# A hybrid attention and DeltaNet block on one core: f32 probabilities times values, and four value projections as seven half-size products

## The chip, the core and the metric

The kernel runs on one core of a Trainium2 chip. The core has five engines with instruction streams of their own: TensorE (PE in the profile; its weight loads are PEld), VectorE (DVE), ScalarE (ACT), GpSimd (POOL) and SyncE (SP). TensorE multiplies a stationary operand (`lhsT`, loaded first) with a moving one (`rhs`) and adds the result into a bank of PSUM; VectorE and ScalarE bring results from there to SBUF. The engines wait for one another through semaphores, and transfers run on DMA queues that SP, ACT and POOL issue.

The metric is the device time of one execution in microseconds. It is compared by the median of several runs.

## The reference

One layer with two token mixers side by side, on 1024 tokens of width 1024. The part that the change touches is mixer A, the dilated windows of attention. Three groups of eight heads (head width 64) have windows and dilations (128, 1), (512, 4) and (2048, 16); in each group the tokens of one residue are cut into blocks of 128 queries, which look at their own block of keys and the one before.

```python
proj = h @ w_in[layer]                       # q, k, v of three groups, gates, and mixer B's inputs
...
scores = jnp.einsum('brnqhd,brnkhd->brnhqk', qb, kb) * (dh ** -0.5)
...
m = jnp.max(scores, axis=-1, keepdims=True)
p = jnp.exp(scores - m)
den = jnp.sum(p, axis=-1, keepdims=True)
o = jnp.einsum('brnhqk,brnkhd->brnqhd', p / den, vb)
lse = (m + jnp.log(den))[..., 0].transpose(0, 1, 2, 4, 3)
...
wts = jax.nn.softmax(jnp.stack(lses), axis=0)
o = jnp.einsum('gbsh,gbshd->bshd', wts, jnp.stack(outs))
```

Mixer B is a gated delta rule with a short convolution, evaluated in chunks. Both outputs are gated, projected up, merged, projected once more and added to the input; a final RMSNorm follows. Everything is float32.

## The kernel before

**Products from f16 parts.** TensorE's operands in the projections are pairs of f16 tensors: a high part and a low part that holds what the high one leaves over. A product takes three passes, high by high, high by low and low by high (`mm3_steps`, lines 183 to 185). The normalised input is `h_hi` and `h_lo`, times 16; weights are `whi` and `wlo`, times 256, made by ScalarE (high) and VectorE (low) from a staged f32 block.

**Units.** The columns of the input projection are cut into units of 256 columns. Attention has 18: for each of three groups `g` (0: undilated, 1: dilation 4, 2: dilation 16, which is worked as residues of 8 with a mask) and two half sets of four heads `hs`, one for queries, one for keys, one for values. A `Feed` object yields a unit's matmuls in steps and prepares the next unit's weights ahead. A `Normal` unit has 32 steps. A `Seven` unit (28 steps) writes its product as two by two blocks and takes seven products of half blocks instead of eight: the four weight blocks are combined into seven (`Seven.split`: sums by VectorE at line 329, splits at lines 330 and 331), the combined inputs are kept once (`sums`), and partial results are copied between PSUM banks (line 367) or kept in SBUF (`x7`) and subtracted as the blocks come out. `SEVENS` lists the units that are done so: before the change, queries and keys of groups 1 and 0, three gate units and four `z` units.

**A value unit** (`v_unit`) has tokens on the partitions: `h` is stationary and the weights move, 256 columns at a time (`gen`). Each PSUM bank is brought out as `Vh` (ScalarE, line 730) and `Vl` (VectorE, line 731), both f16 and scaled to 16 times the value. There is a `gen7` with `by_token` too, which no unit uses before the change: there a product has four groups of tokens, each with 4 × 3 passes of 128 columns.

**Attention** (`att_run`) goes through a set (`g`, `hs`) in 16 steps, one for each block of queries and parity of heads, two heads in each. Three stages are staggered by a step each. `scores` multiplies queries and keys (lines 790 and 792); VectorE adds the mask and takes the row's extreme (line 799), ScalarE the exponential with its sum (line 803), which leaves probabilities in f32 (`sm`). `turn` transposes them on TensorE (line 813), one 128×128 piece for each head and key block, and splits them into `th` (ScalarE, line 818) and `tl` (VectorE, line 819, in the profile under the helper's line 86). `values` multiplies them with the values, three passes of 64 columns for each head and key block. A step has one key block (`nk` = 1) in group 2 and at the start of a residue, two elsewhere. Between the stages TensorE's program takes steps of the feed, as many as the pace gives, so that projections of the next set fill the time in which the other engines work on the present one. The order of TensorE's program is as written; the other engines' is put in order by the planner, by priority.

**Merging.** Results of groups 2 and 1 go to DRAM; for group 0 `combine` reads them back, weighs the three and divides by their common denominator and by the factor 16 of the values (line 885).

**After attention** come mixer B's preparation (from about 545 us), its scan over chunks with the `z` units between, and the output projections.

```python
PE.matmul(out, lhsT=th[:, c], rhs=Vh[:, b, vs], start=(hd == 0 and i == 0), stop=False,
          skip_group_check=True)
PE.matmul(out, lhsT=th[:, c], rhs=Vl[:, b, vs], start=False, stop=False,
          skip_group_check=True)
PE.matmul(out, lhsT=tl[:, c], rhs=Vh[:, b, vs], start=False, stop=(i == nk - 1),
          skip_group_check=True)
```

Of the kernel before, what the change touches and what calls it, by code (L numbers as in the profile page):

```python
# [18 lines left out]
S = 1024  # L19
# [3 lines left out]
H_SCALE = 16.0  # L23
W_SCALE = 256.0
P_SCALE = 1.0 / (H_SCALE * W_SCALE)
# [8 lines left out]
def att_unit(g, hs, what):  # L34
    return U_ATT + (g * 2 + hs) * 3 + what


def gdn_unit(hb, what):
# [2 lines left out]

RUNS = 32
RUNS7 = 28
SEVENS = ([att_unit(g, hs, w) for g in (1, 0) for hs in range(2) for w in range(2)]
          + [U_GATE + i for i in (0, 6, 7)] + [U_Z + i for i in range(4)])
SOLVE_LATER = 1500
SILU = ((1, 2), (0, 0), (1, 0))
# [30 lines left out]
def hybrid_block(ctx: ExitStack, tc: tile.TileContext, A):  # L78
    nc = tc.nc
    V, SC, PE, GP = nc.vector, nc.scalar, nc.tensor, nc.gpsimd  # L80

    def STT(out, in0, scalar, in1, op0, op1, eng=None):
        (eng or V).scalar_tensor_tensor(out, in0, scalar, in1, op0=op0, op1=op1)  # L83

    def TT(out, in0, in1, op, eng=None):
        (eng or V).tensor_tensor(out, in0, in1, op)  # L86
# [9 lines left out]
    start = [ctx.enter_context(ExitStack()) for _ in range(2)]  # L96
# [399 lines left out]
    with tc.manual_schedule(engines={nc.vector.engine, nc.scalar.engine}):  # L496
# [8 lines left out]
        pts = turn_rows(0)  # L505
# [27 lines left out]
        pts = turn_rows(3)  # L533
# [45 lines left out]
    ap = att.enter_context(tc.tile_pool(name="att", bufs=1, side="right"))  # L579
# [15 lines left out]
    def rope_room():  # L595
        return rp.tile([128, 2, 512], F32, name="rx", tag="rx", bufs=2)
# [37 lines left out]
    def rope_tiles():  # L634
        return {n: rp.tile([128, 2, S], F16, name=f"pc{n}", tag=f"pc{n}", bufs=1) for n in "hl"}
# [31 lines left out]

    def rope_first(g, ws, pieces):

        pts = [rope_tiles(), {n: ap.tile([128, 2, S], F16, name=f"pk{n}", tag="V" + n, bufs=2) for n in "hl"}]  # L670

        def half(pt, banks, hf, *offset):
            x = rope_room()
            for ct, p in enumerate(banks):
                rope_evict(g, x, p, ct, *offset)
            rope_half(g, pt, hf, x, *offset)

        for pt, banks in zip(pts, qk):
            half(pt, banks, 0, 0)
        ab = [q, [bank("S", 2), bank("S", 2)]]  # L680
        for i, u in ((2, 1), (3, 0), (3, 1)):
            for ct in range(2):
                quarter(ab[u][ct], ws[u], ct, i)
            if u == 0:

                with tc.high_priority():
                    for n in range(2):
                        feed.units[0][1].split(n)
        for pt, banks in zip(pts, ab):
            half(pt, banks, 1)  # L690
        for pt, pc in zip(pts, pieces):
            rope_out(pt, pc)
# [16 lines left out]

    def v_unit(g, tiles):  # L710
        def start():
            vs = [ap.tile([128, 8, 256], F16, name=n, tag=n, bufs=2) for n in ("Vh", "Vl")]
            tiles().extend(vs)
            return vs

        def gen(w):
            wh, wl = w
            Vh, Vl = start()
            for jj in range(4):
                p = bank("mm", 3)  # L720
                for u in range(2):
                    j = 2 * jj + u
                    for i, _ in enumerate(mm3_steps(
                            p[:, u * 256:u * 256 + 256], (lambda k: tok(g, h_hi, k, j), lambda k: tok(g, h_lo, k, j)),
                            (lambda k: wh[:, k], lambda k: wl[:, k]), first=(u == 0))):
                        if u == 1 and i == KT - 1:
                            with tc.high_priority():
                                vh = Vh[:, 2 * jj:2 * jj + 2].rearrange("p a b -> p (a b)")
                                vl = Vl[:, 2 * jj:2 * jj + 2].rearrange("p a b -> p (a b)")
                                SC.activation(vh, p, AF.Copy, scale=H_SCALE * P_SCALE)  # L730
                                STT(vl, p, H_SCALE * P_SCALE, vh, ALU.mult, ALU.subtract)
                        if i % 2:
                            yield

        def gen7(w):
            vs = start()

            def out(c, hf, p, rest):
                cs = slice(128 * c, 128 * c + 128)
                vh, vl = [v[:, 4 * hf:4 * hf + 4, cs] if g == 0 else  # L740
                          v.rearrange("p (r h) c -> p r h c", h=2)[:, :, hf, cs] for v in vs]
                p = p.rearrange("p (i c) -> p i c", c=128)
                with tc.high_priority():
                    if rest is not None:
                        rest = rest.rearrange("p (i c) -> p i c", c=128)
                        x = rope_room()[:, 0].rearrange("p (i c) -> p i c", c=128)
                        STT(x, p, -1.0, rest, ALU.mult, ALU.subtract)
                        p = x
                    SC.activation(vh, p, AF.Copy, scale=H_SCALE * P_SCALE)
                    STT(vl, p, H_SCALE * P_SCALE, vh, ALU.mult, ALU.subtract)  # L750

            yield from seven_products(w, out, by_token(g))

        return gen, gen7
# [2 lines left out]

    def att_run(g, hs, ts, pace):

        Qh, Ql, K, Vh, Vl = ts  # L760
        steps = [(j, par) for j in range(8) for par in range(2)]
        osbs, Ps, ths, pos = {}, {}, {}, {}
        if (g, hs) == sets[-1]:

            room = ap.tile([128, 2048], F32, name="osbs", tag="Ks", bufs=2)
# [40 lines left out]
        def turn(s):  # L806
            nk = len(blocks(steps[s][0]))
            P = Ps.pop(s)
            pt = bank("G", 2)
            for u in range(2):  # L810
                for i in range(nk):
                    c = (u * nk + i) * 128
                    PE.transpose(pt[:, c:c + 128], P[:, u, i * 128:i * 128 + 128], ident)  # L813
            n = 256 * nk
            th = ap.tile([128, 512], F16, name="th", tag="th", bufs=2)
            tl = ap.tile([128, 512], F16, name="tl", tag="tl", bufs=2)
            with tc.high_priority():
                SC.copy(th[:, :n], pt[:, :n])  # L818
                TT(tl[:, :n], pt[:, :n], th[:, :n], ALU.subtract)
            ths[s] = th, tl  # L820

        def values(s):
            j, par = steps[s]
            kb = blocks(j)
            nk = len(kb)
            th, tl = ths.pop(s)
            if par == 0:
                pos[j] = bank("O", 1)
            po = pos[j]
            for u in range(2):  # L830
                hd = 2 * u + par
                out = po[:, hd * 64:hd * 64 + 64]
                vs = slice(hd * 64, hd * 64 + 64)
                for i, b in enumerate(kb):
                    c = slice((u * nk + i) * 128, (u * nk + i) * 128 + 128)
                    PE.matmul(out, lhsT=th[:, c], rhs=Vh[:, b, vs], start=(hd == 0 and i == 0), stop=False,
                              skip_group_check=True)
                    PE.matmul(out, lhsT=th[:, c], rhs=Vl[:, b, vs], start=False, stop=False,
                              skip_group_check=True)
                    PE.matmul(out, lhsT=tl[:, c], rhs=Vh[:, b, vs], start=False, stop=(i == nk - 1),  # L840
                              skip_group_check=True)
            if par == 0:
                return
            osb = osbs.pop(j)
            SC.copy(osb[:, :256], po[:, :256])
            if g == 1:
                dst = dram[g, hs].rearrange("(n r) c -> r n c", r=4)[j // 2, 128 * (j % 2):128 * (j % 2) + 128]
                nc.scalar.dma_start(out=dst, in_=osb)
            elif g == 2:
                nc.scalar.dma_start(out=dram[g, hs].rearrange("(n r) c -> r n c", r=8)[j], in_=osb)  # L850
            else:
                feed.later(TURN_LAG, combine(hs, j, osb))

        n = len(steps)
# [11 lines left out]
    def combine(hs, j, osb):  # L866
# [8 lines left out]
        f = ap.tile([128, 3, 4], F32, name="f", tag="f", bufs=2)  # L875
        mx = ap.tile([128, 3, 4], F32, name="mx", tag="mx", bufs=2)
# [5 lines left out]
        TT(mx[:, 1], sml[:, 0], sml[:, 1], ALU.add)  # L882
        TT(mx[:, 1], mx[:, 1], sml[:, 2], ALU.add)
        V.reciprocal(mx[:, 2], mx[:, 1])
        STT(f, f, 1.0 / H_SCALE, mx[:, 2:3].to_broadcast([128, 3, 4]), ALU.mult, ALU.mult)

        def hv(x):
            return x.rearrange("p (h v) -> p h v", v=64)
# [88 lines left out]
    tiles = {}  # L977
# [695 lines left out]
    for t in range(8):  # L1673
# [373 lines left out]
```

## Time and profile before

| what | value |
|---|---|
| median of 3 runs | 1074.25 us (1074.08 to 1074.3) |
| the profiled execution's own time | 1076.42 us |
| its span on the core | 1074.6 us |
| mean granted clock of TensorE | 0.997 |
| from HBM, to HBM | 91.13 MB, 36.90 MB |

The profile is of one execution, so sums made from its rows stand beside 1076.42 us. An instruction's group is shown by its line, engine, operation and the tiles that it writes and reads; a `x` number is a count of instructions. Durations of matmuls overlap, since TensorE starts the next before the last has ended, and their ends are modelled: the pace of a stream is read from the starts. A line can be a helper's: 83 and 86 are the kernel's short forms for VectorE operations, so there the tiles tell the group. "Idle before" is idle time of an engine just ahead of an instruction, with what ended it.

### The profile page before, as it was taken

Reading aid. Unit: us, or ns where it says so; the run is one execution under the profiler, and the core shown is the slowest. Engines: PE = TensorE matmul, PEld = TensorE weight load, DVE = VectorE, ACT = ScalarE, POOL = GpSimd, SP = SyncE. Lnnn points to the kernel's source line nnn. Section 1 sums busy time; section 2 is a strip of 40 time slices with the busy share of each in tenths; the row PEclk is TensorE's granted clock in tenths of the full one; section 3 lists DMA queues with packets and bytes.
Section 4 is the critical chain, followed back from the end, with each engine's and each line's share of the span. In section 5 each row is a group of like instructions: output and inputs, shape, how many; then the busy total and the mean of one; then the engine's idle time right before and its main releaser. Section 6 shows DMA issues by size and latency. Waiting matters only on the chain.

```text
span 1074.6 us, 23700 instructions
## 1 busy us (share of the span) xinstructions
PE 1048.8 (98%) x9410; PEld 640.7 (60%) x9410; DVE 864.8 (80%) x1986; ACT 560.9 (52%) x1274; POOL 56.3 (5%) x107
## 2 busy tenths in 40 slices
PE   7999999999999999999999999999999999999997
PEld 5994685775956855765645545555555555444444
DVE  6997997869879779979966997986488679899844
ACT  6455766566666656547735733234344346343523
POOL 0000000000000000000000000110200000000000
PEclk9999999999999999999999999999999999999999
DMA  8144531632625432641234357786685433763132
GB/s 278 60 133 103 139 104 54 171 98 87 181 69 154 108 103 63 177 115 46 76 123 165 84 130 205 237 240 164 184 267 174 140 99 116 286 209 123 48 131 79
DMA packets 99776, 148.47 MB, mean 138 GB/s; under 512 B 31168, under 2 KB 64704, under 8 KB 98512
## 3 DMA queue, kind: packets, MB, share of 16 engines
q1 hardware_dynamic: 69264, 84.64, 27.3%
q0 software_dynamic: 12320, 44.11, 13.1%
q10 hardware_dynamic: 18080, 18.20, 4.9%
q8 instruction: 74, 1.21, 0.5%
q14 instruction: 38, 0.31, 0.1%
HBM read 91.13 MB, written 36.90 MB: 119 GB/s over the span
## 4 chain that ended last, share of the span: by engine, by line
PE 60%; DVE 27%; ACT 5%; issue 3%; DMA 3%; SPq 1%; ACTq 0%; DVEq 0%
PE ps_mm L183 14%; PE ps_mm L184 14%; PE ps_mm L185 14%; DVE ca L83 4%; DVE wlo L83 2%; DVE X L86 2%; DVE stmp L86 2%; DVE sm L799 2%; PE ps_S L185 2%; PE ps_S L184 2%; PE ps_S L183 2%; DVE tl L86 1%; PE ps_G L813 1%; DVE rt L86 1%; ACT sm L803 1%
## 5 line engine op out<-in xcount | busy, mean ns | idle before, releaser
L185 PE MATMUL ps_mm<-h_hi,wlo 128*128 128x512 f16 (+1 forms) x552 | 207.9, 377 | 0.0
L183 PE MATMUL ps_mm<-h_hi,whi 128*128 128x512 f16 (+1 forms) x492 | 185.5, 377 | 0.0
L184 PE MATMUL ps_mm<-h_lo,whi 128*128 128x512 f16 (+1 forms) x492 | 185.3, 377 | 0.0
L185 PEld LDWEIGHTS <-wlo 128*128 128x128 f16 x788 | 77.2, 98 | 86.5 <-issue 0.7
L183 PEld LDWEIGHTS <-whi 128*128 128x128 f16 x848 | 83.3, 98 | 69.1 <-issue 0.6
L184 PEld LDWEIGHTS <-whi 128*128 128x128 f16 x848 | 83.1, 98 | 67.9 <-issue 0.9
L183 PE MATMUL ps_mm<-whi,h_hi 128*128 128x256 f16 x384 | 105.1, 274 | 0.0
L185 PE MATMUL ps_mm<-whi,h_lo 128*128 128x256 f16 x384 | 104.7, 273 | 0.0
L184 PE MATMUL ps_mm<-wlo,h_hi 128*128 128x256 f16 x384 | 104.7, 273 | 0.0
L803 ACT ACTIVATE sm<-sm,osb 128x128 f32<-128x128 f32 (+1 forms) x160 | 69.5, 435 | 65.3 <-DVE osb L799 58.7
L86 DVE TENSOR_TENSOR tl<-ps_G,th 128x256 f16<-128x256 f32 (+1 forms) x96 | 51.8, 539 | 22.1 <-ACT th L818 21.6
L799 DVE CUSTOM_DVE_ANT_0 sm<-ps_S,amask 128x128 f32<-128x128 f32 (+1 forms) x192 | 59.2, 345 | 6.0 <-PE ps_S L792 5.9
L83 DVE SCALAR_TENSOR_TENSOR wlo<-wstage,whi 128x1024 f16<-128x1024 f32 x50 | 60.9, 1217 | 3.4 <-ACT whi L166 3.2
L83 DVE SCALAR_TENSOR_TENSOR ca<-xc,cw,ca 128x512 f32<-128x512 f32 x72 | 53.8, 747 | 5.5 <-ACT ca L1010 4.8
L166 ACT ACTIVATE whi<-wstage 128x1024 f16<-128x1024 f32 x49 | 51.4, 1051 | 1.7 <-ACT gst L948 0.8
L813 PE MATMUL ps_G<-cons,sm 128*128 128x128 f32 x280 | 47.9, 275 | 3.2 <-ACT sm L803 1.5
L83 DVE SCALAR_TENSOR_TENSOR whi<-wstage,whi 128x512 f16<-128x512 f32 x60 | 40.8, 687 | 12.3 <-ACT whi L330 11.7
L330 ACT ACTIVATE whi<-wstage 128x512 f16<-128x512 f32 x60 | 37.1, 626 | 19.6 <-DVE wstage L329 13.3
L813 PEld LDWEIGHTS ps_G<-cons,sm 128*128 128x128 f32 x280 | 35.5, 141 | 19.4 <-ACT sm L803 5.0
L184 PEld LDWEIGHTS <-h_hi 128*128 128x128 f16 x384 | 45.8, 119 | 1.6
L183 PE MATMUL ps_mm<-h_hi,wlo 128*128 128x512 f16 x120 | 45.6, 380 | 1.0 <-DVE rx L83 1.0
L183 PEld LDWEIGHTS <-h_hi 128*128 128x128 f16 x384 | 45.5, 119 | 1.5
(459 smaller groups left out, 2595.7 us busy)
## 6 DMA issues: line engine op xcount, KB each, us to landing
wstage<-in_w POOLq DMA_DIRECT2D x68, 512.0 KB, 4.5
og<-osb ACTq DMA_DIRECT2D x32, 132.0 KB, 2.2
og<-og SPq DMA_DIRECT2D x32, 132.0 KB, 2.2
gspb<-gst ACTq DMA_DIRECT2D x16, 256.0 KB, 2.4
sga<-gspa SPq DMA_DIRECT2D x8, 512.0 KB, 6.5
wstage<-in_w_up POOLq DMA_DIRECT2D x8, 512.0 KB, 4.7
wos<-in_w_out SPq DMA_DIRECT2D x8, 512.0 KB, 5.3
sgb<-gspb SPq DMA_DIRECT2D x8, 512.0 KB, 4.9
```

Of the source, the lines that this page charges most:

```text
L83: (eng or V).scalar_tensor_tensor(out, in0, scalar, in1, op0=op0, op1=op1)
L86: (eng or V).tensor_tensor(out, in0, in1, op)
L166: in_turn(SC.activation(hi[:, 4 * c:4 * c + 4], st, AF.Copy, scale=W_SCALE))
L183: PE.matmul(out, lhsT=wh(k), rhs=mh(k), start=first and i == 0, stop=False, skip_group_check=True)
L184: PE.matmul(out, lhsT=wh(k), rhs=ml(k), start=False, stop=False, skip_group_check=True)
L185: last_pe[0] = PE.matmul(out, lhsT=wl(k), rhs=mh(k), start=False, stop=last and i == len(ks) - 1, skip_group_check=True).ins.name
L330: in_turn(SC.activation(t[:, b, 0], self.part[name], AF.Copy, scale=W_SCALE))
L799: V.tensor_tensor_reduce(P[:, u, :128 * nk], psc[:, u * 256:u * 256 + 128 * nk], mask, -cexp, -NEG, ALU.add, ALU.min, accum_out=osb[:, 256 ...
L803: SC.activation(P[:, u, :128 * nk], P[:, u, :128 * nk], AF.Exp, bias=osb[:, 256 + hd:257 + hd], scale=-1.0, accum_out=osb[:, 260 + hd:261 ...
L813: PE.transpose(pt[:, c:c + 128], P[:, u, i * 128:i * 128 + 128], ident)
```

## The change

The values and the turned probabilities are kept in f32, each as one tensor, and their product is one f32 matmul for each head and key block instead of three f16 passes. The split into `Vh` and `Vl` and that into `th` and `tl` are gone; the scale 1/4096 of the projections goes into the last factor of `combine`. The value units of groups 1 and 0, four in all, join the list `SEVENS`. The memory of `pk`, used once at the start, is now a view of a `vals` buffer, as it was of `Vh` and `Vl` buffers.

```diff
-SEVENS = ([att_unit(g, hs, w) for g in (1, 0) for hs in range(2) for w in range(2)]
+SEVENS = ([att_unit(g, hs, w) for g in (1, 0) for hs in range(2) for w in range(3)]
           + [U_GATE + i for i in (0, 6, 7)] + [U_Z + i for i in range(4)])
...
-        pts = [rope_tiles(), {n: ap.tile([128, 2, S], F16, name=f"pk{n}", tag="V" + n, bufs=2) for n in "hl"}]
+        pk = ap.tile([128, 8, 256], F32, name="pk", tag="vals", bufs=2).rearrange("p a b -> p (a b)").bitcast(F16)
+        pk = pk.rearrange("p (l a s) -> p l a s", l=2, a=2)
+        pts = [rope_tiles(), {n: pk[:, i] for i, n in enumerate("hl")}]
...
-            vs = [ap.tile([128, 8, 256], F16, name=n, tag=n, bufs=2) for n in ("Vh", "Vl")]
-            tiles().extend(vs)
-            return vs
+            v = ap.tile([128, 8, 256], F32, name="vals", tag="vals", bufs=2)
+            tiles().append(v)
+            return v
...
-                                SC.activation(vh, p, AF.Copy, scale=H_SCALE * P_SCALE)
-                                STT(vl, p, H_SCALE * P_SCALE, vh, ALU.mult, ALU.subtract)
+                                SC.copy(v[:, 2 * jj:2 * jj + 2].rearrange("p a b -> p (a b)"), p)
...
                 with tc.high_priority():
-                    if rest is not None:
-                        rest = rest.rearrange("p (i c) -> p i c", c=128)
-                        x = rope_room()[:, 0].rearrange("p (i c) -> p i c", c=128)
-                        STT(x, p, -1.0, rest, ALU.mult, ALU.subtract)
-                        p = x
-                    SC.activation(vh, p, AF.Copy, scale=H_SCALE * P_SCALE)
-                    STT(vl, p, H_SCALE * P_SCALE, vh, ALU.mult, ALU.subtract)
+                    if rest is None:
+                        SC.copy(dst, p)
+                    else:
+                        STT(dst, p, -1.0, rest.rearrange("p (i c) -> p i c", c=128), ALU.mult, ALU.subtract)
...
-            th = ap.tile([128, 512], F16, name="th", tag="th", bufs=2)
-            tl = ap.tile([128, 512], F16, name="tl", tag="tl", bufs=2)
+            PT = ap.tile([128, 512], F32, name="PT", tag="PT", bufs=2)
             with tc.high_priority():
-                SC.copy(th[:, :n], pt[:, :n])
-                TT(tl[:, :n], pt[:, :n], th[:, :n], ALU.subtract)
-            ths[s] = th, tl
+                SC.copy(PT[:, :n], pt[:, :n])
+            PTs[s] = PT
...
-                    PE.matmul(out, lhsT=th[:, c], rhs=Vh[:, b, vs], start=(hd == 0 and i == 0), stop=False,
-                              skip_group_check=True)
-                    PE.matmul(out, lhsT=th[:, c], rhs=Vl[:, b, vs], start=False, stop=False,
-                              skip_group_check=True)
-                    PE.matmul(out, lhsT=tl[:, c], rhs=Vh[:, b, vs], start=False, stop=(i == nk - 1),
+                    PE.matmul(out, lhsT=PT[:, c], rhs=vals[:, b, vs], start=(hd == 0 and i == 0), stop=(i == nk - 1),
                               skip_group_check=True)
...
-        STT(f, f, 1.0 / H_SCALE, mx[:, 2:3].to_broadcast([128, 3, 4]), ALU.mult, ALU.mult)
+        STT(f, f, P_SCALE, mx[:, 2:3].to_broadcast([128, 3, 4]), ALU.mult, ALU.mult)
```

More of the change, by code (lines that the diff above doesn't have):

```diff
@@ L711, in start @@
         def start():
-            vs = [ap.tile([128, 8, 256], F16, name=n, tag=n, bufs=2) for n in ("Vh", "Vl")]
-            tiles().extend(vs)
-            return vs
+            v = ap.tile([128, 8, 256], F32, name="vals", tag="vals", bufs=2)
+            tiles().append(v)
+            return v
         def gen(w):
             wh, wl = w
-            Vh, Vl = start()
+            v = start()
             for jj in range(4):
@@ L727, in gen @@
                             with tc.high_priority():
-                                vh = Vh[:, 2 * jj:2 * jj + 2].rearrange("p a b -> p (a b)")
-                                vl = Vl[:, 2 * jj:2 * jj + 2].rearrange("p a b -> p (a b)")
-                                SC.activation(vh, p, AF.Copy, scale=H_SCALE * P_SCALE)
-                                STT(vl, p, H_SCALE * P_SCALE, vh, ALU.mult, ALU.subtract)
+                                SC.copy(v[:, 2 * jj:2 * jj + 2].rearrange("p a b -> p (a b)"), p)
                         if i % 2:
@@ L735, in gen7 @@
         def gen7(w):
-            vs = start()
+            v = start()
             def out(c, hf, p, rest):
                 cs = slice(128 * c, 128 * c + 128)
-                vh, vl = [v[:, 4 * hf:4 * hf + 4, cs] if g == 0 else
-                          v.rearrange("p (r h) c -> p r h c", h=2)[:, :, hf, cs] for v in vs]
+                dst = (v[:, 4 * hf:4 * hf + 4, cs] if g == 0 else
+                       v.rearrange("p (r h) c -> p r h c", h=2)[:, :, hf, cs])
                 p = p.rearrange("p (i c) -> p i c", c=128)
                 with tc.high_priority():
-                    if rest is not None:
-                        rest = rest.rearrange("p (i c) -> p i c", c=128)
-                        x = rope_room()[:, 0].rearrange("p (i c) -> p i c", c=128)
-                        STT(x, p, -1.0, rest, ALU.mult, ALU.subtract)
-                        p = x
-                    SC.activation(vh, p, AF.Copy, scale=H_SCALE * P_SCALE)
-                    STT(vl, p, H_SCALE * P_SCALE, vh, ALU.mult, ALU.subtract)
+                    if rest is None:
+                        SC.copy(dst, p)
+                    else:
+                        STT(dst, p, -1.0, rest.rearrange("p (i c) -> p i c", c=128), ALU.mult, ALU.subtract)
             yield from seven_products(w, out, by_token(g))
@@ L758, in att_run @@
     def att_run(g, hs, ts, pace):
-        Qh, Ql, K, Vh, Vl = ts
+        Qh, Ql, K, vals = ts
         steps = [(j, par) for j in range(8) for par in range(2)]
-        osbs, Ps, ths, pos = {}, {}, {}, {}
+        osbs, Ps, PTs, pos = {}, {}, {}, {}
         if (g, hs) == sets[-1]:
@@ L825, in values @@
             nk = len(kb)
-            th, tl = ths.pop(s)
+            PT = PTs.pop(s)
             if par == 0:
```

## The prediction

> **What bounds the kernel now.** I read the page first, then the busy time by stretches, then the chain of waits inside the attention part.
>
> ```profile
> PE 1048.8 (98%) x9410; PEld 640.7 (60%) x9410; DVE 864.8 (80%) x1986; ACT 560.9 (52%) x1274; POOL 56.3 (5%) x107
> PE 60%; DVE 27%; ACT 5%; issue 3%; DMA 3%; SPq 1%; ACTq 0%; DVEq 0%
> ```
>
> TensorE (PE) is busy 98% of the span. VectorE (DVE) holds 27% of the chain, so the next question is whether DVE bounds the stretch that the change touches. In this view the columns are the stretch, its length, and the busy time (with instruction count) of PE, PEld, DVE, ACT and POOL, then the granted clock, DMA share and GB/s.
>
> ```profile
> 90.00:545.00 455.00, 447.54 (x3762) 304.52 (x3761) 386.66 (x1039) 289.70 (x776) 18.92 (x36) 1.00 0.38 108
> ```
>
> ```profile
> 200.00:250.00 50.00, 50.00 (x438) 38.48 (x436) 38.05 (x94) 30.72 (x86) 1.06 (x2) 1.00 0.37 97
> ...
> 450.00:500.00 50.00, 47.15 (x496) 32.80 (x494) 42.86 (x153) 29.79 (x78) 2.12 (x4) 1.00 0.33 92
> 500.00:545.00 45.00, 43.00 (x360) 26.84 (x359) 43.41 (x152) 31.04 (x87) 1.44 (x3) 1.00 0.23 72
> ```
>
> Attention with its projections runs from about 90 to 545 us. PE is busy 447.54 of these 455 us, all 50 of the stretch from 200 to 250, and idle 7.5 us in all, most of it after 450. DVE is busy 386.66 us. So PE's own instructions set the pace here: microseconds added to PE's stream appear in the time one for one, while those taken from DVE give back at most the PE idle that DVE causes. That idle is small:
>
> ```profile
> PE ps_O L840 <- DVE tl L86: 2.7, 3, 1.3
> ...
> PE ps_G L813 <- ACT sm L803: 1.5, 4, 0.6
> PE ps_G L813 <- DVE tl L86: 1.2, 1, 1.2
> ```
>
> Of PE's waits (total us, times, longest), 2.7 + 1.2 = 3.9 us end on the low part `tl`, which the change deletes.
>
> **The values products.** Each head and block of keys has three f16 passes now (L836, L838, L840).
>
> ```profile
> L838 PE MATMUL ps_O<-Vl,th 128*128 128x64 f16 x280 | 35.0, 193 | 0.0
> ```
>
> ```profile
> L818 ACT CAST th<-ps_G x96: 346/374/592, 102.5 to 542.8; 128x256 f16<-128x256 f32 x52, 128x512 f16<-128x512 f32 x44
> ```
>
> The line has 280 passes, so there are 840 f16 passes in 96 groups: 52 groups with one key block for two heads (128x256 turned) and 44 with two blocks (128x512); 52×2 + 44×4 = 280. The durations of matmuls overlap, so I take the pace from starts. In the chain, in order of time, one group of six passes stands between two projections:
>
> ```profile
> 252.12 0.03 PE ps_O L836
> ...
> 252.26 0.03 PE ps_O L840
> 252.29 0.22 PE ps_mm L183
> ```
>
> Six passes from 252.12 to 252.29 are 0.029 us each, and 840 × 0.029 = 24.4 us now.
>
> After the change each of the 280 is one f32 matmul, 128x128 stationary by 128x64 moving. The trace has that very form at L1120 and L1121, one f32 matmul each, recorded as x2:
>
> ```profile
> 500.68 0.33 PE L1120 MATMUL ps_G<-bg,cons 128*128 128x64 f32 x2
> 500.85 0.39 PE L1121 MATMUL ps_G<-bg,cons 128*128 128x64 f32 x2
> 501.07 0.38 PE L183 MATMUL ps_mm<-h_hi,whi 128*128 128x512 f16 x1
> ```
>
> So one f32 matmul is two passes. The first pair costs 0.17 us (as I read it, its first load lies behind the 512-column pass ahead), a following pair 0.22 us, two matmuls 0.39 us. A group with one key block is exactly these two matmuls; one with two blocks is four, 0.17 + 3×0.22 = 0.83 us. The sum is 52×0.39 + 44×0.83 = 20.3 + 36.5 = 56.8 us, against 24.4: **+32.4 us** of PE. Fewer passes (560 for 840), but each is almost four times as long in the stream.
>
> The FP8 and Floating Point Precision page of the Trainium skill (TensorE Precision Notes) says that true f32 takes four passes through the array. The trace shows two load and matmul records for each; were it four, the values groups alone would come to about 118 us, which is a rival below.
>
> The bounds of the f32 pass are 0.034 us below, from 64x64 f32 passes of the scan, of which 30 follow one another in 1.02 us, and 0.11 us above. I take the upper, since form and neighbours are the same.
>
> ```profile
> 795.36 1.02 PE ps_G L1734 x30
> ```
>
> **The value projections.** Four of six V units become seven half-size products. A V unit now is 192 passes of 256 columns (384 of each of three kinds over six units); a new one is 7 products × 4 token groups × 4 k × 3 = 336 passes of 128 columns.
>
> ```profile
> L183 PE MATMUL ps_mm<-whi,h_hi 128*128 128x256 f16 x384 | 105.1, 274 | 0.0
> ```
>
> ```profile
> 274.61 0.27 PE L183 MATMUL ps_mm<-whi,h_hi 128*128 128x256 f16 x1
> ...
> 275.92 0.60 PE L813 MATMUL ps_G<-cons,sm 128*128 128x128 f32 x4
> ```
>
> ```profile
> 30.80 0.61 PE L478 MATMUL ps_S<-h_hi,whi 128*128 128x128 f16 x8
> 31.25 0.61 PE L478 MATMUL ps_S<-h_lo,whi 128*128 128x128 f16 x8
> 31.70 0.61 PE L478 MATMUL ps_S<-h_hi,wlo 128*128 128x128 f16 x8
> ```
>
> Twelve 256-column passes start between 274.61 and 275.92: 0.109 us each, 20.9 us for a unit. Sixteen 128-column passes take 31.70 − 30.80 = 0.90 us: 0.056 us each, 18.8 us for a unit. The saving is 2.1 us a unit, **−8.4 us** for four.
>
> A half-size pass leaves half the time to hide its load. For the group with dilation 4 the loads step over columns, and are longer:
>
> ```profile
> L185 PEld LDWEIGHTS <-h_lo x47: 112/114/118, 270.6 to 289.8; 128*128 128x128 f16 x47
> ```
>
> ```profile
> L184 PEld LDWEIGHTS <-h_hi x25: 97/98/98, 350.0 to 359.9; 128*128 128x128 f16 x25
> ```
>
> The 16 ns more (114 against 98) are hidden under 256 columns; under 128 columns the trace doesn't show them. Bounds: nothing if still hidden, 16 ns × 672 passes of two units = 10.8 us if not. A 98 ns load already hides under a 0.029 us pass, and here there are 0.056 us, so I take nothing.
>
> TensorE: Matmul & The Clock Gate (Trainium skill, Back-to-back issue gap) speaks against this part: it gives about 81 ns for a 128-column pass in a stream with loads. By that figure a unit is 27.2 us, slower than now, and four cost 33.6 us more than in my sum. The trace has 56 ns with a load ahead of every pass at L478, so the trace decides.
>
> **What moves on the other engines.** None of this is on the path while PE is full.
>
> ```profile
> L86 DVE TENSOR_TENSOR tl<-ps_G,th 128x256 f16<-128x256 f32 (+1 forms) x96 | 51.8, 539 | 22.1 <-ACT th L818 21.6
> L83 DVE SCALAR_TENSOR_TENSOR Vl<-ps_mm,Vh 128x512 f16<-128x512 f32 x24 | 16.5, 687 | 7.3 <-ACT Vh L730 7.3
> L83 DVE SCALAR_TENSOR_TENSOR wlo<-wstage,whi 128x1024 f16<-128x1024 f32 x50 | 60.9, 1217 | 3.4 <-ACT whi L166 3.2
> L166 ACT ACTIVATE whi<-wstage 128x1024 f16<-128x1024 f32 x49 | 51.4, 1051 | 1.7 <-ACT gst L948 0.8
> L83 DVE SCALAR_TENSOR_TENSOR whi<-wstage,whi 128x512 f16<-128x512 f32 x60 | 40.8, 687 | 12.3 <-ACT whi L330 11.7
> L329 DVE TENSOR_TENSOR wstage<-wstage 128x512 f32<-128x512 f32 x60 | 40.7, 685 | 0.4
> L330 ACT ACTIVATE whi<-wstage 128x512 f16<-128x512 f32 x60 | 37.1, 626 | 19.6 <-DVE wstage L329 13.3
> L367 ACT COPY ps_mm<-ps_mm 128x512 f32<-128x512 f32 x30 | 17.2, 574 | 23.1 <-PE ps_mm L185 22.6 <-ACT osb L845 0.4
> ```
>
> DVE loses 96 `tl` (51.8 us) and 24 `Vl` (16.5 us). It gains the weight work of four units, each seven splits and four sums for two wide splits: 7×0.687 + 4×0.685 − 2×1.217 = 5.1 us, 20.5 for four; and two evictions a unit that subtract the kept product, 8 × 0.69 = 5.5 us. Net −42 us. ACT gains 4 × (7×0.626 − 2×1.051) = 9.1 us of splits and 12 copies between banks at 0.574 (6.9 us), and loses 8 of its 24 V evictions (4.7 us): +11 us on an engine that is busy 289.70 of 455. The f32 copies `PT` take the place of `th` with the same source and shape; I cost them equal. What hides the splits is PE's stream ahead of each unit, 28 steps long, as it does for the query and key units of the same groups now. Without that cover a unit would wait for one split and its copy, 0.69 + 0.63 = 1.3 us, 5.2 us for four. Loads stay two of 512 KB a unit on POOL's queue, SP's queue has the same transfers, and the new buffers take as many bytes as the old. No wait is added: the values product waits for ACT's copy alone, one DVE step earlier.
>
> What that gives back is a wait on `tl` at L840 (2.7 us) and at L813 (1.2 us). Late next there are the copy by ACT and the exponentials (`sm`), 1.5 us, of which I count nothing. I take **−4 us**; the bounds are 0 and all 7.5 us of idle.
>
> **Sum.** +32.4 − 8.4 − 4.0 = +20.0 us. The profiled execution took 1076.42 us (span 1074.6 and 1.8 around it), so it would give 1096.4; its 2.2 us above the median of 1074.25 I leave out, and the forecast is **1094.3 us**.
>
> **The rivals.**
> - *Faster: f32 passes that overlap.* The first pass of L1120 took only 0.056 us of stream. If all 560 did, because loads slip behind earlier passes, the values cost 31.4 us, +7.0, and the total is 7.0 − 8.4 − 4.0 = −5.4: 1068.9 us. It decides at (24.4 + 8.4 + 4.0)/560 = 0.066 us a pass. Against it: the following pair shows 0.11 us a pass. Chance 0.06, of which 0.01 for a pass so near 0.066 us that nothing can be measured.
> - *DVE's relief is worth more.* PE's modelled ends cover short stalls, so true idle may be twice the 7.5 us; with 42 us less on DVE all 15 could go: 32.4 − 8.4 − 15 = +9.0, 1083.3 us. For it: DVE 43.41 of 45 us in the last stretch. Against: with PE full from 200 to 250 there is nothing to give back there. Chance 0.10.
> - *Strided loads show.* +10.8 us on the forecast: 1105.1 us. Chance 0.06.
> - *Four passes for f32.* Each matmul counts as two of the pairs above: a group of one block 0.17 + 3×0.22 = 0.83 us, of two 0.17 + 7×0.22 = 1.71 us, together 118.4 us, 94.0 more than now: 1155.9 us. The x2 at L1120 speaks against it. Chance 0.02.
>
> **How the numbers follow.** The forecast keeps 0.76. Its own range, 1088 to 1101, comes from the idle given back (0 to 7.5 us), the splits uncovered (0 to 5.2 us), and pairs read to 0.01 us (44 groups × 0.03 = 1.3 us). The range for 8 in 10 reaches down towards the case of DVE's relief and up short of the strided loads: 1086 to 1103. A measurement tells 0.2% (2.1 us) from no change. Only the first rival is faster, 0.05, or within 0.2%, 0.01; slower holds 0.94.
>
> **What would show it.** In the profile after: L836's successor x560 with f32 forms, starts 0.11 us apart; 128-column V passes 0.056 us apart, also in the group with dilation 4; DVE about 42 us less busy; attention ending near 565 instead of 545 us; and later stretches of unchanged length. A start distance near 0.06 us in the values, or V passes of 0.07 us, would make it wrong, and so would attention that ends at 555, with PE's waits gone.

## The result and the profile after

The changed kernel takes 1091.54 us (median of 4, 1090.75 to 1092.13) beside 1074.28 us before: a ratio of 1.0154, with a 95% interval of 1.0136 to 1.0172, so it is 17.3 us slower. The two profiled executions differ by a little less, 1091.44 against 1076.42 us with spans of 1089.7 and 1074.6, since that of before lay above its median. Sums made from these two traces explain their 15 us; by the medians the change costs 2.3 us more, and no trace shows in which stretch.

The page of the changed kernel, busy time and chain:

```profile
PE 1071.0 (98%) x9706; PEld 676.0 (62%) x9706; DVE 833.5 (76%) x1910; ACT 575.4 (53%) x1298; POOL 56.4 (5%) x107
...
PE 81%; DVE 13%; ACT 3%; issue 2%; DMA 2%; SPq 0%; ACTq 0%; DVEq 0%
```

TensorE holds 81% of the chain instead of 60%, VectorE 13% instead of 27%: the kernel has become more PE-bound, by PE's own work. Stretches of the changed kernel (length, then busy PE, PEld, DVE, ACT, POOL), the attention part first, which now ends near 561 us:

```profile
98.20:561.20 463.00, 462.00 (x4031) 336.48 (x4030) 356.18 (x983) 302.05 (x798) 18.55 (x35) 1.00 0.37 105
...
560.00:755.00 195.00, 194.95 (x1855) 102.62 (x1854) 149.77 (x289) 80.68 (x140) 16.65 (x30) 1.00 0.60 175
755.00:915.00 160.00, 156.86 (x2142) 83.75 (x2141) 114.25 (x257) 70.57 (x121) 12.86 (x23) 0.99 0.51 161
915.00:1089.70 174.70, 168.03 (x807) 78.80 (x804) 133.61 (x264) 70.75 (x157) 3.18 (x6) 0.99 0.41 144
```

The same stretches of before, cut at 545, 740 and 900 us, were 195, 160 and 174.6 us long:

```profile
545.00:740.00 195.00, 194.32 (x1855) 101.95 (x1855) 154.97 (x314) 80.64 (x141) 16.80 (x31) 1.00 0.62 177
740.00:900.00 160.00, 156.84 (x2140) 83.91 (x2139) 114.01 (x256) 70.60 (x121) 12.85 (x23) 0.99 0.51 160
900.00:1074.60 174.60, 168.00 (x807) 78.80 (x804) 133.46 (x264) 70.84 (x157) 3.18 (x6) 0.99 0.41 145
```

They hold the same numbers of passes within two and are merely moved by 15 us. So all of the change lies in attention. PE is idle there for 1 us of 463, where it was idle for 7.5 of 447.6 (97.7 to 545.3 us), both by modelled ends.

The values products, first by form, then as two groups in the chain and one in the timeline:

```profile
L830 PE MATMUL ps_O<-vals,PT 128*128 128x64 f32 x560 | 74.3, 268 | 0.0
```

```profile
251.48 0.84 PE ps_O L830 x8
252.32 0.21 PE ps_mm L183
...
256.21 0.39 PE ps_O L830 x4
256.60 0.22 PE ps_mm L183
```

```profile
277.91 0.22 PE L185 MATMUL ps_mm<-whi,h_lo 128*128 128x128 f16 x1
277.96 0.61 PE L830 MATMUL ps_O<-vals,PT 128*128 128x64 f32 x4
278.41 0.22 PE L183 MATMUL ps_mm<-whi,h_hi 128*128 128x128 f16 x1
```

There are 560 records, two for each of 280 products; they are called passes here. Eight of them take 0.84 us and four 0.39 us behind a 512-column pass; behind a 128-column pass of a V unit four take 278.41 − 277.96 = 0.45 us, since less of the first load is covered.

What remains is a sum over starts. I took every PE pass from the first scores pass to the pass after the last values pass, gave each the time to the next start, and counted as a **stall** what a pass took beyond the pace of its kind by more than 0.06 us. This measure sees short waits that modelled ends cover.

```
us in attention        before   after   difference
values                   24.5    58.7     +34.2
V units (five of six)   105.2    96.0      -9.2
turn                     31.1    30.8      -0.3
scores, other units     276.0   276.0       0.0
stalls                   10.9     1.6      -9.2
total                   447.6   463.1     +15.5
```

The first V unit runs ahead of this stretch. The f32 products cost 34.2 us, the seven products save 9.2 us, and 9.2 us of waiting went away.

### The profile page after: what moved, and what is told of

Read it like the earlier page. It is cut to its first block, busy times and chain, and to the rows that moved or that the text cites. A ratio compares the mean times of both kernels' runs of the same rounds, so it can differ in the third digit from the quotient of the medians.

```text
span 1089.7 us, 24260 instructions
## 1 busy us (share of the span) xinstructions
PE 1071.0 (98%) x9706; PEld 676.0 (62%) x9706; DVE 833.5 (76%) x1910; ACT 575.4 (53%) x1298; POOL 56.4 (5%) x107
## 4 chain that ended last, share of the span: by engine, by line
PE 81%; DVE 13%; ACT 3%; issue 2%; DMA 2%; SPq 0%; ACTq 0%; DVEq 0%
PE ps_mm L183 19%; PE ps_mm L185 18%; PE ps_mm L184 18%; PE ps_O L830 5%; DVE ca L83 3%; PE ps_G L809 3%; DVE X L86 2%; DVE stmp L86 2%; PE ps_S L185 2%; PE ps_S L183 2%; PE ps_S L184 2%; PE ps_S L786 1%; PE ps_S L788 1%; DVE wlo L83 1%; PE ps_G L185 1%
## 5 line engine op out<-in xcount | busy, mean ns | idle before, releaser
L83 DVE SCALAR_TENSOR_TENSOR whi<-wstage,whi 128x512 f16<-128x512 f32 x76 | 52.1, 689 | 39.5 <-ACT whi L330 39.3
L830 PEld LDWEIGHTS ps_O<-vals,PT 128*128 128x128 f32 x560 | 74.3, 191 | 7.8
L830 PE MATMUL ps_O<-vals,PT 128*128 128x64 f32 x560 | 74.3, 268 | 0.0
L330 ACT ACTIVATE whi<-wstage 128x512 f16<-128x512 f32 x76 | 47.2, 627 | 22.5 <-DVE wstage L329 14.4
L184 PE MATMUL ps_mm<-wlo,h_hi 128*128 128x256 f16 (+1 forms) x256 | 57.3, 246 | 0.0
L329 DVE TENSOR_TENSOR wstage<-wstage 128x512 f32<-128x512 f32 x76 | 52.1, 686 | 0.8
L813 ACT COPY PT<-ps_G 128x256 f32<-128x256 f32 (+1 forms) x96 | 44.3, 461 | 7.3 <-PE ps_G L809 7.0
L809 PE MATMUL ps_G<-cons,sm 128*128 128x128 f32 x280 | 46.7, 274 | 0.7 <-ACT sm L799 0.6
L183 PE MATMUL ps_mm<-whi,h_hi 128*128 128x256 f16 (+1 forms) x192 | 46.2, 255 | 0.0
L185 PE MATMUL ps_mm<-whi,h_lo 128*128 128x256 f16 (+1 forms) x192 | 46.2, 255 | 0.0
L184 PE MATMUL ps_mm<-h_lo,wlo 128*128 128x512 f16 x120 | 45.5, 379 | 0.0
```

The costliest lines, as they stand in the source:

```text
L183: PE.matmul(out, lhsT=wh(k), rhs=mh(k), start=first and i == 0, stop=False, skip_group_check=True)
L184: PE.matmul(out, lhsT=wh(k), rhs=ml(k), start=False, stop=False, skip_group_check=True)
L185: last_pe[0] = PE.matmul(out, lhsT=wl(k), rhs=mh(k), start=False, stop=last and i == len(ks) - 1, skip_group_check=True).ins.name
L329: in_turn(V.tensor_tensor(self.part[name], self.part[x], self.part[y], ALU.add))
L330: in_turn(SC.activation(t[:, b, 0], self.part[name], AF.Copy, scale=W_SCALE))
L813: SC.copy(PT[:, :n], pt[:, :n])
```

## The experiments

The question was the last line but one: what took the waiting away, and does each half of the change pay alone? Theory A: VectorE's split of the probabilities and values made PE wait, by its time and its place in the chain. Rival B: the longer f32 passes give the other engines more time for each step. Rival C: the seven products change the order of the feed.

All runs in one table, by the same sum over starts. "DVE" is VectorE's busy share of the attention stretch; stalls include passes at half clock behind a long wait (last section). The kernel before was run beside each group; its medians were 1074.12 us (e1 to e4), 1075.17 (e5 to e8) and 1073.78 (e9 to e11).

```
run                          values  V units  stalls  DVE   median us   ratio to before, 95%
before                         24.5   105.2    10.9   85%   1074.28
after                          58.7    96.0     1.6   77%   1091.54     1.0154 [1.0136, 1.0172]
e1 f32 only                    57.4   104.8     1.1   72%   1101.69     1.0255 [1.0240, 1.0270]
e2 sevens only                 24.9    97.4    24.6   88%   1083.70     1.0096 [1.0073, 1.0118]
e3 after + VectorE step        58.8    96.0     4.9   84%   1094.84     1.0197 [1.0177, 1.0216]
e4 one f16 pass, sevens         8.1    96.4    22.5   80%   1062.46     0.9887 [0.9862, 0.9913]
e5 before + filler passes      57.1   105.2     9.3   81%   1110.14     1.0335 [1.0316, 1.0354]
e6 one f16 pass, no sevens      8.1   105.2     6.6   77%   1059.21     0.9856 [0.9840, 0.9871]
e7 e2, sums on GpSimd          24.9    96.4    37.2   83%   1099.70     1.0233 [1.0216, 1.0249]
e8 after in float32r              -       -       -     -   1074.54     0.9992 [0.9980, 1.0003]
e9 the same once more             -       -       -     -   1074.24     1.0003 [0.9990, 1.0016]
e10 e8, no sevens                 -       -       -     -   1070.28     0.9965 [0.9952, 0.9977]
e11 before, no low parts       24.4   105.2     5.4   75%   1068.88     0.9957 [0.9943, 0.9972]
```

**e1: the f32 values alone.** In the changed kernel the value units are taken out of the list again:

```diff
-SEVENS = ([att_unit(g, hs, w) for g in (1, 0) for hs in range(2) for w in range(3)]
+SEVENS = ([att_unit(g, hs, w) for g in (1, 0) for hs in range(2) for w in range(2)]
```

> The f32 values alone; all six V units stay Normal. PE's attention stream gains 34.2 us over before (values 24.5 to 58.7 us). Theory A (the 9.2 us of PE stalls that vanished were caused by VectorE's split of the probabilities, by its time and by its place in the chain): stalls stay near 1.6 us, 1074.3 + 34.2 - 9.2 = 1099 us. Rival C (the stalls went because seven products for V changed the order of the feed): stalls are back at 10.9 us, 1108 us.

Measured: 1101.69 us, stalls 1.1 us. Rival C is out: the stalls vanish without the seven products. Against the changed kernel it also shows that with f32 values the seven products are worth 1101.69 − 1091.54 = 10 us. Of these, 469.9 − 463.1 = 6.8 us lie in attention; the rest lies behind it, where the program is the same (PE's longest wait there is 3.8 us at L1256 in e1 and 2.3 us in the changed kernel).

**e2: the seven products alone.** The opposite edit of the same line, in the kernel before.

> The four V units as seven products alone; values stay three f16 passes with th, tl, Vh and Vl. PE saves 9.2 us of stream; VectorE gains some 20 us of weight work and 5.5 us of evictions on top of before, and keeps tl and Vl. Theory A: stalls stay at 10.9 us or grow by as much again as VectorE's load grows: between 1065 us (stalls as before) and 1075 us (all given back). Rival C: stalls fall to 1.6 us as well, 1074.3 - 9.2 - 9.2 = 1056 us.

Measured: 1083.70 us, worse than the bad end of the range of A. The passes saved are there (V units 105.2 to 97.4 us), but stalls grew from 10.9 to 24.6 us. PE's longest waits in e2 inside attention (total us, times, longest):

```profile
PE ps_G L899 <- DVE osb L86: 5.5, 1, 5.5
...
PE ps_O L840 <- DVE tl L86: 3.1, 5, 0.9
...
PE ps_G L813 <- ACT sm L803: 2.3, 6, 0.6
...
PE ps_mm L183 <- DVE Vl L83: 1.6, 3, 0.7
```

The longest, 5.5 us at L899, is the transpose of merged outputs, which waited for VectorE's merging; three of the four end on VectorE. So the same edit costs 9.6 us here and gains 10 us beside f32 values; by the traces of attention alone it costs 454.5 − 447.6 = 6.9 us here and gains 6.8 us there.

**e3: a VectorE step put back into the changed kernel.**

```diff
                 SC.copy(PT[:, :n], pt[:, :n])
+                TT(PT[:, :n], pt[:, :n], PT[:, :n], ALU.max)
```

> The changed kernel, with one VectorE operation put back behind ScalarE's copy of the turned probabilities: PT = max(ps, PT) in place, which changes no value, has tl's inputs and shape, and stands between copy and product as tl did (96 times, about 0.54 us). PE's stream is that of the changed kernel. Theory A: the stalls come back, up to 9 us: about 1100 us, with values and turn waiting for VectorE. Rival B (the longer f32 passes give the other engines time, whatever VectorE does): at most 2 us more than the changed kernel, 1091 to 1094 us.

The step has the duration that `tl` had (first row e3, second row the kernel before):

```profile
L86 DVE TENSOR_TENSOR PT<-ps_G,PT x96: 392/425/692, 103.2 to 562.0; 128x256 f32<-128x256 f32 x52, 128x512 f32<-128x512 f32 x44
```

```profile
L86 DVE TENSOR_TENSOR tl<-ps_G,th x96: 393/425/692, 102.9 to 544.2; 128x256 f16<-128x256 f32 x52, 128x512 f16<-128x512 f32 x44
```

Measured: 1094.84 us, stalls 4.9 us, 3.3 more in both. That is a third of the 9.2 us and between the two theories: the step matters, but it does not bring all back. The second eviction of the values, `Vl`, was not put back.

**e4: short passes, with VectorE relieved.** The changed kernel with `PT` and `vals` in f16 (`pk`, which shared the memory of `vals`, gets its own).

```diff
-            v = ap.tile([128, 8, 256], F32, name="vals", tag="vals", bufs=2)
+            v = ap.tile([128, 8, 256], F16, name="vals", tag="vals", bufs=2)
...
-            PT = ap.tile([128, 512], F32, name="PT", tag="PT", bufs=2)
+            PT = ap.tile([128, 512], F16, name="PT", tag="PT", bufs=2)
```

> The changed kernel with the turned probabilities and the values each as one f16 tensor, so one f16 pass of 0.029 us instead of one f32 matmul of two; it leaves out the low parts of both. PE's values come to 280 x 0.029 = 8.2 us instead of 58.7. If stalls stay as small as in the changed kernel (theory A: VectorE's split was their cause): 1091.5 - 50.5 = 1041 us. Rival B (the long passes gave the others time): stalls of 10.9 us or more are back, 1050 us or more.

Measured: 1062.46 us. The values fell to 8.1 us as expected, but 21 of the 50 us came back as stalls. Theory A alone would have left them at 1.6. The longest wait, 3.6 us at L809 for the exponentials, lies in this stretch (columns: stretch, length, busy PE, PEld, DVE, ACT, POOL, granted clock, DMA share, GB/s):

```profile
468.00:472.00 4.00, 0.37 (x2) 0.14 (x1) 3.96 (x10) 2.10 (x6) 0.53 (x1) 1.00 0.38 111
```

VectorE is busy all through it, with weights and mixer B's preparation, and the row's extreme that the exponentials need comes behind them. In e2 it was likewise busy for all 5.4 us of the wait at L899. In these two cases PE waits for what stands just ahead of a step in VectorE's order, which a share over the whole stretch doesn't show.

**e5: a longer PE stream, with VectorE's load as before.**

```diff
                     PE.matmul(out, lhsT=tl[:, c], rhs=Vh[:, b, vs], start=False, stop=(i == nk - 1),
                               skip_group_check=True)
+                    for _ in range(4):
+                        PE.matmul(po[:, 256 + hd * 64:320 + hd * 64], lhsT=th[:, c], rhs=Vh[:, b, vs], start=False,
+                                  stop=True, skip_group_check=True)
```

> The kernel before (f16 parts, th and tl, all V units Normal), with four more f16 passes for each head and key block into unused columns of the same bank: work for nothing, 1120 x 0.029 = 32.7 us of PE stream, about what the f32 products add, and VectorE's load is that of before. Theory B (a longer PE stream covers the waits for the other engines): stalls fall from 10.9 to about 4 us or less, as in e3, and the time is 1074.1 + 32.7 - 7 = 1100 us or less. Theory A (stalls come of VectorE's split alone): stalls stay, 1106.8 us.

Measured: 1110.14 us, stalls 9.3 us. The filler took its 32.6 us in full, and 1.5 us of stalls went. The profiled execution was the fastest of the four, at 1107.28 us; the median lies 35 us above before, so there even the 1.5 us don't show. Rival B alone is out as well: with Normal V units, length without relief buys almost nothing.

**e11: relief for VectorE, with PE's passes as before.** The counterpart of e5.

```diff
-                                STT(vl, p, H_SCALE * P_SCALE, vh, ALU.mult, ALU.subtract)
...
-                TT(tl[:, :n], pt[:, :n], th[:, :n], ALU.subtract)
...
-                    PE.matmul(out, lhsT=th[:, c], rhs=Vl[:, b, vs], start=False, stop=False,
+                    PE.matmul(out, lhsT=th[:, c], rhs=Vh[:, b, vs], start=False, stop=False,
...
-                    PE.matmul(out, lhsT=tl[:, c], rhs=Vh[:, b, vs], start=False, stop=(i == nk - 1),
+                    PE.matmul(out, lhsT=th[:, c], rhs=Vh[:, b, vs], start=False, stop=(i == nk - 1),
```

> The kernel before without VectorE's tl and Vl: the product of the high parts is taken three times (and divided by three in the merging), so the low parts of probabilities and values are left out, PE's stream is that of before, pass for pass, and VectorE has 68 us less to do. Theory A (VectorE's split causes the stalls): stalls fall from 10.9 to under 3 us, 1066 us. Theory B (only a longer PE stream covers them): 1072 us or more.

Measured: 1068.88 us, stalls 5.4 us, a loss of 5.5. Theory A has the larger part, and misses its own number (under 3). Of the 5.4 us that are left, 1.8 are a single wait at L1070, for ScalarE's copy of a result out of PSUM, and about 1 us is in 512-column passes at half clock soon after it (last section). So, with Normal V units: relief alone takes 5.5 us of stalls (e11), length alone 1.5 (e5), both together 9.7 (e1). Relief has by far the larger part.

**e6 and e7: what a unit of seven products costs.** e6 is e4 with Normal V units. e7 is e2 with the sums of weight blocks moved:

```diff
-                    in_turn(V.tensor_tensor(self.part[name], self.part[x], self.part[y], ALU.add))
+                    in_turn(GP.tensor_tensor(self.part[name], self.part[x], self.part[y], ALU.add))
```

> e4 with the four V units Normal again; it leaves out the low parts of probabilities and values, as e4 does. PE's stream is 9.2 us longer than e4's, VectorE's load about 26 us lower. If a unit of seven only pays while VectorE has time to spare (theory B: a balance of the two streams), stalls fall from e4's 22.5 us by about as much as in e2 against before (13.7 us) and the time is 1062.5 + 9.2 - 13.7 = 1058 us. If the stalls of e4 come from the short values stream alone, they stay: 1071.7 us.

> e2 (sevens alone, f16 parts) with the sums of weight blocks of all Seven units on GpSimd instead of VectorE: 76 sums, 52 us less on VectorE in the whole kernel. If VectorE's weight work is what ate the saving of e2, stalls in attention fall from 24.6 us to about 10 us and the time is 1070 us or less. If GpSimd's sums take much longer than VectorE's 0.69 us, the splits come late and PE waits for weights instead: 1084 us or more.

e6 measured 1059.21 us with stalls of 6.6 us: without the four units, 9 us more of passes and 16 us less of stalls than e4, as expected. e7 went the other way, 1099.70 us with stalls of 37.2 us. A sum takes 1.28 us on GpSimd, 0.68 on VectorE (e7, then e2):

```profile
L329 POOL TENSOR_TENSOR wstage<-wstage x76: 1257/1277/1818, 151.4 to 910.0; 128x512 f32<-128x512 f32 x76
```

```profile
L329 DVE TENSOR_TENSOR wstage<-wstage x76: 656/684/694, 151.4 to 902.3; 128x512 f32<-128x512 f32 x76
```

That weights came late is not what the trace shows: none of the waits of PE that the profile lists in attention ends on a weight split. They end on the exponentials (7.8 us), on evictions by VectorE into `rx` (6.2 us) and on `tl` (6.0 us). VectorE itself got little relief. The 52 sums of attention took 35.5 us of it in e2, but its busy time there fell only from 399.9 to 386.5 us, since other steps of VectorE grew longer (e7, then e2):

```profile
L83 DVE SCALAR_TENSOR_TENSOR wlo<-wstage,wlo 128x512 f16<-128x512 f32 x57 | 50.3, 892 | 3.5 <-ACT wlo L330 2.5
```

```profile
L83 DVE SCALAR_TENSOR_TENSOR wlo<-wstage,wlo 128x512 f16<-128x512 f32 x57 | 38.2, 684 | 0.8
```

In e7 the 28 of these splits that met no sum on GpSimd took 683 ns in the mean, the 29 that overlapped one 1093 ns; `tl`, which reads PSUM, took 0.68 us (128x512) either way. So e7 says nothing on what a true relief would bring. VectorE's share is not the whole story anyway: e4 stalls for 22.5 us with VectorE 80% busy, the kernel before for 10.9 us at 85%.

**e8 to e10: the changed kernel in float32r.** (`pk` is declared likewise.)

```diff
-            v = ap.tile([128, 8, 256], F32, name="vals", tag="vals", bufs=2)
+            v = ap.tile([128, 8, 256], mybir.dt.float32r, name="vals", tag="vals", bufs=2)
...
-            PT = ap.tile([128, 512], F32, name="PT", tag="PT", bufs=2)
+            PT = ap.tile([128, 512], mybir.dt.float32r, name="PT", tag="PT", bufs=2)
```

> The changed kernel with PT and vals declared float32r instead of float32, the same bytes and the same program otherwise. If a product is then one pass, the values stream falls from 58.7 us to between 280 x 0.029 = 8.2 and 280 x 0.112 = 31.4 us, and the time from 1091.5 to between 1041 and 1064 us plus the stalls that a shorter stream lays bare (up to e4's 22.5 us): 1062 to 1075 us. If it is two passes as for f32: 1091.5 us.

> e8 again, for a profile of an undisturbed execution: 1074.5 us. One load and one matmul for each of the 280 products; by the time of e8, a values stream of about 30 us (0.11 us a product) with stalls of about 10 us, or of 8 us with stalls of 30.

> e8 with the four V units Normal: PE's stream 9.2 us longer, VectorE's load some 26 us lower. If seven products pay only where VectorE has time to spare (they gave -10 us with f32 products, +10 us with f16 parts, +3 us with one f16 pass), at e8's stream they give back more than they save: 1065 to 1074 us. If they pay, 1080 us or more.

e8 measured 1074.54 us, e9 1074.24, e10 1070.28. The timeline of e9 shows a group of two key blocks:

```profile
257.60 0.38 PE L185 MATMUL ps_mm<-h_hi,wlo 128*128 128x512 f16 x1
257.63 0.72 PE L830 MATMUL ps_O<-vals,PT 128*128 128x64 f32 x4
258.19 0.39 PE L183 MATMUL ps_mm<-h_hi,wlo 128*128 128x512 f16 x1
```

The trace now has one load and one matmul for a product: four in 258.19 − 257.60 − 0.22 = 0.37 us (0.22 is the pace of the 512-column pass ahead), against eight passes in 0.84 us in f32. Starts in these traces overlap the pass ahead, so e8 to e10 are left out of the sum over starts. Float32r takes back the 17 us, and Normal V units in e10 save another 4 us.

An estimate is possible from the rest. Attention takes 444.0 us in e9 and 439.3 in e10. Without the other units and scores (276.0), `turn` (31) and the V units (96 and 105.2) some 41 and 27 us are left for values and stalls together. By the pace of the groups (0.14 to 0.20 us with one key block, 0.37 to 0.42 with two) the values are about 25 us of it, so stalls are about 15 us with the four units of seven and 2 to 3 us without. The units of seven thus add 14 us of stalls beside f16 parts (e2 against before), 16 beside one f16 pass (e4 against e6) and about 13 beside float32r, but 0.5 beside f32 (the changed kernel against e1). VectorE's split is there in the first pair alone, so the split is not what makes these units dear; only the long f32 stream covered them. Between e9 and the changed kernel VectorE does the same work, and length alone decides over some 13 us. With Normal V units relief alone nearly does it: in e10 the values are about as short as in the kernel before, and 2 to 3 us of its 10.9 us of stalls are left.

**A version that beats both.** e6, at 0.9856 [0.9840, 0.9871] of before. It leaves out the low parts of probabilities and values, so it is a less exact product; e10, which keeps four-byte operands, is at 0.9965 [0.9952, 0.9977]. What a float32r product loses in accuracy was not measured.

## Why the prediction came out as it did

The forecast was 1094.3 us in a range of 1086 to 1103; 1091.54 lies in it, and attention bound by PE's own stream was the right reading. Part of the closeness is luck: the values cost more than forecast, and the other two terms saved more. By its steps:

- **The values, +32.4 us: measured +34.2.** Pairs of 0.17 and 0.22 us from L1120 and L1121 were the right model. Most of the rest is the first load, which is less covered in the V units (0.45 instead of 0.39 us for four passes); with Normal V units, in e1, the values took 57.4 us, near the 56.8 of the forecast. The Trainium skill (FP8 and Floating Point Precision, TensorE Precision Notes) has four passes for true f32; the trace has two records for each product, 560 for 280, and doesn't tell how many passes through the array a record is. The 118.4 us of the rival with four such records did not come.
- **The value projections, −8.4 us: measured −9.2.** The 1344 passes of 128 columns took 75.0 us, 0.056 us each, with contiguous and with strided loads alike, so the strided loads stay hidden. The 81 ns of the Trainium skill (TensorE: Matmul & The Clock Gate, Back-to-back issue gap) did not appear.
- **Idle given back, −4 us with bounds of 0 and 7.5: measured −9.2.** This is the term that was mis-sized. It counted only the waits that end on `tl`, 3.9 us, and its bound came from PE's idle by modelled ends, which run past the true pace of a stream. By that measure 7.5 − 1.0 = 6.5 us went, within the bounds; by starts there were 10.9 us to lose and 9.2 went. (By the medians, 2.3 us further apart, some 7 us.) The rival of VectorE's larger relief named that cover, and its 15 us was too much. Of the cause, `tl` was only a part (3.3 us in e3). The forecast counted nothing for the exponentials, and their wait shrank too, from the 1.5 us shown in the prediction to this:

```profile
PE ps_G L809 <- ACT sm L799: 0.6, 1, 0.6
```

- **VectorE's load, −42 us: measured −39 by the sum of durations**, −31 on the page, which counts overlapping instructions once.
- **The faster rival** needed 0.066 us a pass; f32 passes took 58.67/560 = 0.105.
- **What the prediction did not see** is how the halves hang together. It priced the seven products at −8.4 us wherever they stand. That holds beside f32 values (−10 us) and fails alone: e2 is 9.6 us slower than before, with 13.7 us more of stalls for 7.8 us fewer of passes. The stalls go with the length of the stream beside these units, since about as many come without VectorE's split (e4, e9) as with it (e2), and only the f32 passes keep them at 0.5 us. Which part of a seven unit makes PE wait, VectorE's time for it or the order in which its long steps stand ahead of the softmax steps, stays open: no run changed one without the other.

## What to carry to other kernels

Price a change of number format by the starts of a pass of the same shape already in the trace, not by the count of products: two f32 passes of 0.105 us replaced three f16 passes of 0.029 us. Count what a shorter stream had covered before counting what it saves: passes taken from a bound engine can come back as stalls where another engine is busy all through a step that it waits for, so a half of a change can lose alone what it gains beside the other half. Read the idle of a pipelined engine from starts; modelled ends hide short waits.

## What the runs showed of the hardware

A wait of PE can cost more than itself. In e4 PE waited 3.63 us for ScalarE's exponentials, and the granted clock was 0.58 in the 4 us behind it (columns: PE's start and duration; then the stretch as above with the granted clock after POOL):

```profile
471.73 0.72 PE L809 MATMUL ps_G<-cons,sm 128*128 128x128 f32 x2 [3.63 <-ACT sm L799]
...
474.44 0.63 PE L184 MATMUL ps_mm<-h_lo,whi 128*128 128x512 f16 x1
474.86 0.63 PE L185 MATMUL ps_mm<-h_hi,wlo 128*128 128x512 f16 x1
...
476.56 0.38 PE L183 MATMUL ps_mm<-h_hi,whi 128*128 128x512 f16 x1
476.77 0.38 PE L184 MATMUL ps_mm<-h_lo,whi 128*128 128x512 f16 x1
```

```profile
472.00:476.00 4.00, 3.94 (x14) 1.86 (x14) 3.49 (x13) 4.00 (x12) 0.53 (x1) 0.58 0.25 79
```

For that time 512-column passes started 0.42 us apart instead of 0.21, which added some 1.7 us to the wait. TensorE: Matmul & The Clock Gate of the Trainium skill (Part 1) names an idle window of about 3.4 us for a fall to half the clock; this wait agrees. Shorter waits had the same fall behind them, so 3.4 us is not a length below which the clock is safe here. In the kernel before it was a wait of 2.3 us at L1266 (this and the next by modelled ends, like the 3.63), with a granted clock of 0.50 from 764 to 766 us; in e11 one of 1.67 us at L1070, with 0.50 from 466 to 469 us. Both times PE went on with small passes, of 64 columns in the kernel before, of 32 and 16 in e11. No run here tells what these had to do with it.
